# Up-projections of a two-layer encoder on one Trainium2 core: the product of the activation moved to VectorE, weight sums and sums of squares made by adding transfers

## The chip, the cores and the metric

The kernel runs on one core of a Trainium2 chip. The metric is the device time of one execution in microseconds, as a median of several runs. The engines are TensorE (PE in the rows, its weight loads PEld), VectorE (DVE), ScalarE (ACT), GpSimd (POOL) and SyncE (SP), which issues transfers. They run side by side, each in the order of its own queue.

## The reference

The input is `x`, 1024 frames of 1024 channels in float32. Two layers run over it; each adds a mixer and then a gated feed-forward network to the residual stream. The feed-forward network is what the change touches:

```python
def conv_ffn(h, w_up, conv_w, conv_b, w_down):       # h: 1024 x 1024, w_up: 1024 x 5632
    u = h @ w_up
    up = jnp.pad(u, ((0, 0), (CONV_WIDTH - 1, 0), (0, 0)))
    conv = conv_b
    for j in range(CONV_WIDTH):                       # width 3, causal, per channel
        conv = conv + conv_w[j] * up[:, j:j + s]
    a, g = jnp.split(conv, 2, axis=-1)                # 2816 channels each
    return (jax.nn.silu(a) * g) @ w_down
```

`h` is the residual stream after an RMS norm with a gain per channel. The mixer of layer 0 is stick-breaking attention beside a pooling mixer, that of layer 1 gated linear attention.

## The kernel before

Everything lies channels on partitions: a tile of `x` is 128 channels by 1024 frames, and there are 8 of them. Matmuls work on pairs of float32r tiles: a float32 value is cut into a high part (ScalarE, a cast) and a remainder (VectorE, a subtraction), and a product takes three matmuls, high x high, high x low, low x high. Such a cut is called a split.

*The feed-forward loop.* The 5632 up-projected channels are 22 pairs of tiles, one of `a` and one of `g`. The first two pairs are plain projections. From the third on a pair is computed in `class Pair` by a scheme of seven half-size products instead of eight: the weights of the pair and the input are 2 x 2 blocks, and the products P1 to P7 use blocks and sums of blocks. Each product is 12 matmuls of 128x512, 84 for a pair. On the weight side four sums of 128x512 are formed per pair (lines 856, 857, 860 and 861, in `sum12` and `sum34`): `s12[:, T0]`, the two halves of `raw_g` added; `s12[:, T1]`; `s34[:, T0]`; and `s34[:, T1]`, where `T0` and `T1` are the two 512-column halves. They are split into `s12h`, `s12l`, `s34h`, `s34l`; `a22` is the split of one half of `raw_g`, and `whi`, `wlo` that of `wraw` (lines 843, 844). On the input side four sums per channel block are formed once per layer by `rsums` (lines 905 to 908) and split by `rblock`.

The products accumulate in four PSUM banks, named `lin`, `z`, `t` and `d`. ScalarE copies intermediate results out (lines 926, 933, 941), VectorE adds them to others (lines 937, 942, 948, 952) and scales the outputs `u` by the norm's factor (line 911). P3 goes on accumulating in the bank that line 942 has read, so P3 waits for line 942; P7 goes on in the bank that the copy of line 933 has read. Then come the convolution (line 956 on ScalarE, 957 and 959 on VectorE), the SiLU on ScalarE (line 1076), the product with the gate on GpSimd (line 1077) and a store of the result to DRAM. Three tiles `c` serve the two convolutions of a pair in turn. The loads, sums and splits for a pair are made ahead, in the iterations before it (`load_a`, `sum12`, `sum34`, called after the products of the pair).

*The entry.* The last two blocks of the mixer's output projection are added to the residual tiles by `add_tiles` (line 819) in the order `ORDER`, two tiles ahead; for each finished tile `NormBlocks.add` stores it, makes two split blocks (`blk`, lines 289 and 290), squares it (line 309, `ndg` or `nsq` in the rows) and adds the square to `nacc` on VectorE (line 310). The first up-projection of the layer (`first_tile`) runs two tiles behind, between the `add_tiles`. At the end PE sums the squares over channels (`stats`, line 261), ScalarE and VectorE make the factor, VectorE spreads it on a diagonal (line 268), and after the plain projection of tile 1 PE spreads it over the partitions (`spread`, line 275). The outputs of the first projections can only be scaled after that (line 1008).

*The order.* PE runs in the order in which the program names its instructions. All other engines and SP's queue are put in order by a planner, which works through the program's dependences with assumed costs; on the chip that order is fixed. A buffer with several turns is handed on when its last reader is done. The tiles in `xpool` have 11 places: the 8 residual tiles, the sums of squares, temporaries.

Of the kernel before, what the change touches and what calls it, by code (L numbers as in the profile page):

```python
# [56 lines left out]
def trunk_kernel(  # L57
# [220 lines left out]
    class NormBlocks(Norm):  # L278
# [14 lines left out]
        def add(self, m, x):  # L293
            xs[m] = dram.tile([P, T], F32, tag=f"xs{self.layer}_{m}", name="xs")
            nc.sync.dma_start(xs[m], x)
            g = pcol(self.col + m)
            if m < KT // 2:
                self.b11.append(self.block(x[:, 0:512], g))
                self.b12.append(self.block(x[:, 512:T], g))
            else:  # L300
                self.b21.append(self.block(x[:, 0:512], g))
                self.b22.append(self.block(x[:, 512:T], g))
            self.n += 1
            if self.n == 1:
                self.acc = self.acc_tile()
                S.activation(self.acc, x, AF.Square)
            else:
                sq = self.sq_tile()
                S.activation(sq, x, AF.Square)
                V.tensor_tensor(self.acc, self.acc, sq, op=ALU.add)  # L310
            if m < KT // 2:
                S.activation(x, x, AF.Copy, scale=g)
# [514 lines left out]
    def ffn(layer, nm, after, ow, mixt, onward=None):  # L827
# [23 lines left out]
        def load_a(i):  # L851
            raws[i], *A[i] = raw_a(i)
            nc.sync.dma_start(raw_g, wup[layer, FT + i])

        def sum12(i):
            V.tensor_tensor(s12[:, T0], raw_g[:, T0], raw_g[:, T1], op=ALU.add)
            V.tensor_tensor(s12[:, T1], s12[:, T0], raws[i][:, T0], op=ALU.subtract)

        def sum34(i):
            V.tensor_tensor(s34[:, T0], raws[i][:, T0], raw_g[:, T0], op=ALU.subtract)  # L860
            V.tensor_tensor(s34[:, T1], raws[i][:, T1], s12[:, T1], op=ALU.subtract)
# [26 lines left out]

        rhs = {n: [None] * 4 for n in ("T1", "T2", "T3", "T4")}
# [12 lines left out]
        def rsums(k):  # L902

            lo_, hi_, g = x[k], x[k + 4], pcol(nm.col + k + 4)
            V.tensor_tensor(lo_[:, T0], lo_[:, T1], lo_[:, T0], op=ALU.subtract)
            V.scalar_tensor_tensor(lo_[:, T1], hi_[:, T1], g, lo_[:, T1], op0=ALU.mult, op1=ALU.subtract)
            V.scalar_tensor_tensor(hi_[:, T1], hi_[:, T1], g, lo_[:, T0], op0=ALU.mult, op1=ALU.subtract)
            V.scalar_tensor_tensor(hi_[:, T0], hi_[:, T0], g, hi_[:, T1], op0=ALU.mult, op1=ALU.subtract)
# [53 lines left out]

        first = []
# [16 lines left out]
        def plain(i, tags):  # L980
            w, ps = raw_a(i)[1:], [bank(t) for t in tags]
            for n in range(KT):
                plain_tile(w, ps, n)
            return ps

        otags = itertools.cycle("td")
        add_tiles(ow, mixt, otags, ORDER[:2])
        for n, m in enumerate(ORDER):
            if n >= 2:
                add_tiles(ow, mixt, otags, [m])  # L990
            nm.add(m, x[m])
            if n >= 2:
                first_tile(n - 2)
# [4 lines left out]
        first_tile(KT - 2)  # L998
        first_tile(KT - 1)
        nm.stats("t")  # L1000
        ps = plain(1, "td")
        nm.spread(iter("dt"))
# [12 lines left out]
        load_a(2)  # L1015
        split_a22()
        sum12(2)
        sum34(2)
# [16 lines left out]
        for i in range(FT):  # L1035
# [8 lines left out]
            else:  # L1044
                p = Pair(i)
                ua, ug = p.ua, p.ug
                if not nx:
                    first_down()
                p.P1()
                p.P5()  # L1050
                p.P6()
                if nx:
                    split_s12()
# [4 lines left out]
                p.P7()  # L1058
                scaled(ug[:, T1], T1)
# [3 lines left out]
                if nx:  # L1063
                    split_a22()
                scaled(ug[:, T0], T0)
                p.P3()
                if nx:
                    split_s34()
                scaled(ua[:, T1], T1)
            if 0 < i < FT - 2:  # L1070
                load_a(i + 2)
                sum12(i + 2)
                sum34(i + 2)
# [3 lines left out]
            G.tensor_tensor(ca, ca, cg, op=ALU.mult)  # L1077
# [393 lines left out]
```

## Time and profile before

| | |
|---|---|
| median of three runs | 2269.87 us (2266.28 to 2270.54) |
| the profiled execution's own time | 2268.67 us |
| its span, first to last instruction | 2267.0 us |
| PE busy | 2210.9 us (98%) |
| DVE busy | 1644.5 us (73%) |
| ACT busy | 1009.3 us (45%) |
| POOL busy | 305.1 us (13%) |
| mean granted TensorE clock | 0.995 |

The profile is of one execution. Times in its rows count from the start of the span. A busy PE is not PE at its peak, since matmuls overlap; how fast it goes is read from the starts of its instructions. Idle time of an engine that nobody waits for costs nothing. The feed-forward loop of layer 0 lies at about 485 to 894 us, that of layer 1 at 1614 to 2024.

### The profile page before, as it was taken

How to read it: one execution, taken by the hardware profiler on the slowest of the kernel's cores; microseconds unless marked ns; L12 is line 12 of the kernel's file. 1: busy time of each engine (PE TensorE's matmuls, PEld its weight loads, DVE VectorE, ACT ScalarE, POOL GpSimd, SP SyncE). 2: the span in 40 equal slices, each digit the busy share in tenths (PEclk: the TensorE clock that was granted, in tenths of full speed). 3: DMA queues.
4: the chain of work that ended last, by engine and by line, in shares of the span. 5: the costliest groups of instructions: out<-in, count | busy, mean ns of one | idle time of the engine just before them, and what ended most of it. 6: DMA issues, size and time to landing. Idle time of an engine off the chain costs nothing.

```text
span 2267.0 us, 27398 instructions
## 1 busy us (share of the span) xinstructions
PE 2210.9 (98%) x10648; PEld 1822.6 (80%) x10648; DVE 1644.5 (73%) x2244; ACT 1009.3 (45%) x1533; POOL 305.1 (13%) x191
## 2 busy tenths in 40 slices
PE   8999989999999999999999999999999999999999
PEld 7889868777888887888887788787778888878887
DVE  5687688799999998554546555548899999985543
ACT  6666666454444444221256253536544444442210
POOL 2230110001111112321000000000011111133210
PEclk9999999999999999999999999999999999999999
DMA  4132341222222226421101011102222222264312
GB/s 144 58 103 77 110 137 53 107 78 75 84 84 84 84 84 221 151 96 53 30 21 45 29 47 38 47 29 103 75 83 78 81 84 84 84 224 138 102 47 75
DMA packets 56898, 194.26 MB, mean 86 GB/s; under 512 B 6832, under 2 KB 7472, under 8 KB 56768
## 3 DMA queue, kind: packets, MB, share of 16 engines
q1 hardware_dynamic: 56768, 192.51, 26.3%
q8 instruction: 84, 1.38, 0.3%
q14 instruction: 46, 0.38, 0.1%
HBM read 149.49 MB, written 42.99 MB: 85 GB/s over the span
## 4 chain that ended last, share of the span: by engine, by line
PE 83%; DVE 6%; ACT 4%; issue 4%; DMA 2%; POOL 1%; SPq 0%; DVEq 0%; ACTq 0%; POOLq 0%
PE lin L885 13%; PE z L885 9%; PE lin L137 5%; PE lin L139 5%; PE lin L141 5%; PE t L885 4%; PE d L885 4%; PE z L137 3%; PE z L139 3%; PE z L141 3%; PE t L137 3%; PE t L139 3%; PE t L141 3%; PE d L137 2%; PE d L139 2%
## 5 line engine op out<-in xcount | busy, mean ns | idle before, releaser
L123 ACT CAST whi<-wraw 128x1024 fp32r<-128x1024 f32 (+3 forms) x106 | 105.4, 996 | 355.2 <-PE d L139 222.2
L1077 POOL TENSOR_TENSOR c<-c 128x1024 f32<-128x1024 f32 x44 | 109.5, 2490 | 900.5 <-ACT c L1076 884.5
L911 DVE TENSOR_TENSOR u<-u,rstd_bc 128x512 f32<-128x512 f32 x160 | 159.8, 1000 | 2.6
L124 DVE TENSOR_TENSOR wlo<-wraw,whi 128x1024 fp32r<-128x1024 f32 (+2 forms) x92 | 130.5, 1418 | 38.8 <-ACT whi L123 38.2
L956 ACT ACTIVATE c<-u,prm 128x1024 f32<-128x1024 f32 x88 | 109.6, 1245 | 76.5 <-DVE u L911 75.0
L1106 POOL TENSOR_TENSOR act<-a,act 128x1024 fp32r<-128x1024 f32 x40 | 107.1, 2685 | 218.3 <-ACT act L1105 214.2
L137 PE MATMUL lin<-h_hi,whi 128*128 128x512 f32 x304 | 119.9, 433 | 6.3 <-ACT whi L123 6.1
L819 DVE TENSOR_TENSOR x<-x,t 128x512 f32<-128x512 f32 x105 | 71.9, 685 | 64.6 <-PE t L141 64.3
L959 DVE SCALAR_TENSOR_TENSOR c<-u,prm,c 128x1022 f32<-128x1022 f32 x88 | 118.3, 1344 | 0.1
L675 DVE TENSOR_TENSOR_SCAN pt<-pt,z 128x128 f32<-128x128 f32 (+3 forms) x96 | 93.1, 970 | 33.7 <-ACT z L668 32.6
L957 DVE SCALAR_TENSOR_TENSOR c<-u,prm,c 128x1023 f32<-128x1023 f32 x88 | 112.5, 1279 | 6.5 <-ACT c L956 6.4
L885 PE MATMUL d<-T,a 128*128 128x512 f32 x480 | 115.3, 389 | 0.0
L819 DVE TENSOR_TENSOR x<-x,d 128x512 f32<-128x512 f32 x105 | 71.9, 684 | 56.6 <-PE d L141 56.6
L139 PE MATMUL lin<-h_lo,whi 128*128 128x512 f32 x304 | 109.7, 399 | 1.8 <-DVE h_lo L247 1.8
L141 PE MATMUL lin<-h_hi,wlo 128*128 128x512 f32 x304 | 109.6, 399 | 0.0
L885 PE MATMUL z<-blk,s34h 128*128 128x512 f32 x320 | 100.7, 396 | 5.7 <-DVE u L942 5.7
L885 PEld LDWEIGHTS d<-T,a 128*128 128x128 f32 x480 | 90.1, 188 | 18.7
L864 ACT CAST s12h<-s 128x1024 fp32r<-128x1024 f32 x42 | 44.2, 1052 | 135.2 <-PE lin L885 120.3
L885 PE MATMUL lin<-T,s34h 128*128 128x512 f32 x320 | 98.9, 390 | 2.2 <-ACT tm L933 2.2
L885 PE MATMUL z<-blk,s12h 128*128 128x512 f32 x320 | 100.7, 396 | 0.0
L885 PE MATMUL lin<-blk,whi 128*128 128x512 f32 x320 | 99.8, 393 | 0.0
L885 PE MATMUL lin<-T,s12h 128*128 128x512 f32 x320 | 99.5, 392 | 0.0
(429 smaller groups left out, 6334.4 us busy)
## 6 DMA issues: line engine op xcount, KB each, us to landing
wraw<-in_wup SPq DMA_DIRECT2D x44, 512.0 KB, 3.6
act<-c SPq DMA_DIRECT2D x44, 512.0 KB, 2.6
wraw<-in_wdn SPq DMA_DIRECT2D x44, 512.0 KB, 3.9
raw_g<-in_wup SPq DMA_DIRECT2D x40, 512.0 KB, 3.6
a<-act SPq DMA_DIRECT2D x40, 512.0 KB, 4.5
xs<-x SPq DMA_DIRECT2D x16, 512.0 KB, 2.6
x<-xs SPq DMA_DIRECT2D x16, 512.0 KB, 5.0
x<-in_xT SPq DMA_DIRECT2D x8, 512.0 KB, 5.0
```

The costliest lines, as they stand in the source:

```text
L124: (eng or V).tensor_tensor(lo[:, cs], raw[:, cs], hi[:, cs].bitcast(F32), op=ALU.subtract)
L137: PE.matmul(out[i], wh, ah[i], start=first, stop=False)
L139: PE.matmul(out[i], wh, al[i], start=False, stop=False)
L141: PE.matmul(out[i], wl, ah[i], start=False, stop=last)
L819: V.tensor_tensor(x[m][:, cs], x[m][:, cs], pss[m][i], op=ALU.add)
L885: PE.matmul(ps, w, m, start=first and k == 0 and n == 0, stop=k == 3 and n == 2, skip_group_check=True)
L911: V.tensor_tensor(dst, dst, rstd_bc[:, cs], op=ALU.mult)
L956: S.activation(c, u, AF.Identity, scale=pcol(b + 2), bias=pcol(b + 3))
L957: V.scalar_tensor_tensor(c[:, 1:], u[:, :T - 1], pcol(b + 1), c[:, 1:], op0=ALU.mult, op1=ALU.add)
L959: V.scalar_tensor_tensor(c[:, 2:], u[:, :T - 2], pcol(b), c[:, 2:], op0=ALU.mult, op1=ALU.add)
L1077: G.tensor_tensor(ca, ca, cg, op=ALU.mult)
L1106: G.tensor_tensor(t[1], a32, t[0].bitcast(F32), op=ALU.subtract)
```

## The change

Five things change. (1) The product of the activation (line 1077) goes from GpSimd to VectorE. (2) Two of the four weight sums per pair are made by transfers that add to their target, issued from GpSimd's queue: `s12[:, T0]` is loaded with one half of the weights and the other half is added from DRAM; `s34[:, T1]` is loaded with a half and `s12[:, T1]` is added from on-chip memory. (3) To let these be plain additions, the sign of `s12[:, T1]` is turned round, and on the input side the signs in `rsums` with it, with a small tile `ngain` of negated gains. (4) The loads, sums and splits for coming pairs are placed anew, spread over the products of a pair. (5) In the entry, five of the sums of squares are made by adding transfers into one tile, which joins the accumulator at the end; three tiles instead of two are computed ahead; and the spread of the norm's factor goes into the middle of the plain projection.

```diff
@@ NormBlocks.add
+            sq = self.acc_tile() if self.n == 1 else self.sq_tile()
+            S.activation(sq, x, AF.Square)
             if self.n == 1:
-                self.acc = self.acc_tile()
-                S.activation(self.acc, x, AF.Square)
+                self.part = sq
+            elif self.n < KT - 1:
+                G.dma_start(self.part, sq, accum_op=ALU.add)
+            elif self.n == KT - 1:
+                self.acc = sq
             else:
-                sq = self.sq_tile()
-                S.activation(sq, x, AF.Square)
                 V.tensor_tensor(self.acc, self.acc, sq, op=ALU.add)
+                V.tensor_tensor(self.acc, self.acc, self.part, op=ALU.add)
@@ ffn
+        def load_s1(i):
+            nc.sync.dma_start(s12[:, T0], wup[layer, FT + i][:, T0])
+            G.dma_start(s12[:, T0], wup[layer, FT + i][:, T1], accum_op=ALU.add)
+
+        def load_g(i):
+            nc.sync.dma_start(raw_g, wup[layer, FT + i])
+
         def load_a(i):
-            raws[i], *A[i] = raw_a(i)
-            nc.sync.dma_start(raw_g, wup[layer, FT + i])
-
-        def sum12(i):
-            V.tensor_tensor(s12[:, T0], raw_g[:, T0], raw_g[:, T1], op=ALU.add)
-            V.tensor_tensor(s12[:, T1], s12[:, T0], raws[i][:, T0], op=ALU.subtract)
-
-        def sum34(i):
+            raws[i] = wpool.tile([P, T], F32, tag="wraw", name="wraw", bufs=1)
+            nc.sync.dma_start(raws[i], wup[layer, i])
+
+        def load_s4(i):
+            nc.sync.dma_start(s34[:, T1], wup[layer, i][:, T1])
+
+        loads = (load_s1, load_g, load_a, load_s4)
+
+        def sums(i):
+            V.tensor_tensor(s12[:, T1], raws[i][:, T0], s12[:, T0], op=ALU.subtract)
+            G.dma_start(s34[:, T1], s12[:, T1], accum_op=ALU.add)
             V.tensor_tensor(s34[:, T0], raws[i][:, T0], raw_g[:, T0], op=ALU.subtract)
-            V.tensor_tensor(s34[:, T1], raws[i][:, T1], s12[:, T1], op=ALU.subtract)
+
+        def split_a11(i):
+            A[i] = [wpool.tile([P, T], R32, tag=n, name=n) for n in ("whi", "wlo")]
+            split(*A[i], raws[i])
...
+        ngain = small.tile([P, 4], F32, tag="ngain", name="ngain", bufs=1)
+        S.activation(ngain, prm[:, nm.col + 4:nm.col + 8], AF.Copy, scale=-1.0)
@@ rsums
-            V.scalar_tensor_tensor(hi_[:, T1], hi_[:, T1], g, lo_[:, T0], op0=ALU.mult, op1=ALU.subtract)
-            V.scalar_tensor_tensor(hi_[:, T0], hi_[:, T0], g, hi_[:, T1], op0=ALU.mult, op1=ALU.subtract)
+            V.scalar_tensor_tensor(hi_[:, T1], hi_[:, T1], ng, lo_[:, T0], op0=ALU.mult, op1=ALU.add)
+            V.scalar_tensor_tensor(hi_[:, T0], hi_[:, T0], g, hi_[:, T1], op0=ALU.mult, op1=ALU.add)
@@ entry of ffn
+        AHEAD = 3
-        def plain(i, tags):
+        def plain(i, tags, amid=None):
             w, ps = raw_a(i)[1:], [bank(t) for t in tags]
             for n in range(KT):
                 plain_tile(w, ps, n)
+                if n == 4 and amid is not None:
+                    amid()
             return ps
...
-        add_tiles(ow, mixt, otags, ORDER[:2])
+        add_tiles(ow, mixt, otags, ORDER[:AHEAD])
         for n, m in enumerate(ORDER):
-            if n >= 2:
+            if n >= AHEAD:
                 add_tiles(ow, mixt, otags, [m])
             nm.add(m, x[m])
-            if n >= 2:
-                first_tile(n - 2)
+            if n >= AHEAD:
+                first_tile(n - AHEAD)
...
-        first_tile(KT - 2)
-        first_tile(KT - 1)
+        for n in range(KT - AHEAD, KT):
+            first_tile(n)
         nm.stats("t")
-        ps = plain(1, "td")
-        nm.spread(iter("dt"))
+        ps = plain(1, "td", lambda: nm.spread(iter("dt")))
...
-        load_a(2)
+        for ld in loads:
+            ld(2)
         split_a22()
-        sum12(2)
-        sum34(2)
+        sums(2)
+        split_a11(2)
         split_s12()
         split_s34()
@@ the loop over pairs
+                further = i + 2 < FT
                 p.P1()
+                if nx:
+                    sums(i + 1)
                 p.P5()
                 p.P6()
-                if nx:
-                    split_s12()
                 p.P2()
                 scaled(ua[:, T0], T0)
                 if not nx:
                     p.P4()
                 p.P7()
+                if nx:
+                    split_s12()
+                if further:
+                    load_s1(i + 2)
                 scaled(ug[:, T1], T1)
                 if nx:
                     p.P4()
                 p.D21()
                 if nx:
                     split_a22()
+                if further:
+                    load_g(i + 2)
                 scaled(ug[:, T0], T0)
+                if nx:
+                    split_a11(i + 1)
+                if further:
+                    load_a(i + 2)
                 p.P3()
                 if nx:
                     split_s34()
+                if further:
+                    load_s4(i + 2)
                 scaled(ua[:, T1], T1)
-            if 0 < i < FT - 2:
-                load_a(i + 2)
-                sum12(i + 2)
-                sum34(i + 2)
+            if i == 1:
+                for ld in loads:
+                    ld(i + 2)
             conv(FT + i, ug, cg)
             conv(i, ua, ca)
             S.activation(ca, ca, AF.Silu)
-            G.tensor_tensor(ca, ca, cg, op=ALU.mult)
+            V.tensor_tensor(ca, ca, cg, op=ALU.mult)
```

## Rows read from the trace of the kernel before

**Rows 1.** The page, busy time of the engines: microseconds, share of the span, instructions.

```profile
PE 2210.9 (98%) x10648; PEld 1822.6 (80%) x10648; DVE 1644.5 (73%) x2244; ACT 1009.3 (45%) x1533; POOL 305.1 (13%) x191
```

**Rows 2.** Busy time by stage: the stretch, its length, then for PE, PEld, DVE, ACT and POOL the busy microseconds and the number of instructions, then the granted TensorE clock, the busy share of the transfer engines and their GB/s. The first is the entry of layer 0, the second the middle of its loop, the third the end of layer 1's entry.

```profile
424.00:485.00 61.00, 58.45 (x257) 46.51 (x255) 59.23 (x83) 39.67 (x52) 0.00 (x0) 1.00 0.26 95
540.00:870.00 330.00, 330.00 (x1439) 269.95 (x1438) 304.93 (x343) 150.83 (x174) 40.86 (x17) 1.00 0.26 85
...
1591.00:1600.00 9.00, 7.14 (x25) 5.38 (x24) 9.00 (x13) 7.15 (x11) 0.00 (x0) 0.81 0.35 117
```

**Rows 3.** Waits of PE from 424 to 900 us (entry and loop of layer 0): who waited for whom, microseconds in total, times, longest.

```profile
PE z L885 <- DVE u L942: 2.9, 3, 1.4
PE lin L139 <- DVE blk L290: 2.0, 2, 1.2
PE lin L885 <- ACT tm L933: 1.1, 1, 1.1
PE lin L137 <- DVE u L1008: 0.8, 1, 0.8
```

**Rows 4.** Waits of PE from 1557 to 2030 us (entry and loop of layer 1), the same columns. The two lines left out are, word for word, the last two of rows 3.

```profile
PE lin L139 <- DVE blk L290: 3.4, 2, 1.9
PE z L885 <- DVE u L942: 2.7, 2, 1.4
...
```

**Rows 5.** Waits of the weight loads (PEld) from 424 to 900 us, the same columns.

```profile
PEld z L885 <- DVE u L942: 4.2, 3, 1.8
PEld lin L139 <- DVE blk L290: 2.9, 2, 1.7
PEld lin L137 <- DVE u L1008: 1.6, 1, 1.6
PEld lin L885 <- ACT tm L933: 1.5, 1, 1.5
```

**Rows 6.** The timeline of a steady pair of layer 0: start, duration, engine, line, operation, output and inputs, count. The two weight-load rows are the first of P3 in this pair and in the next.

```profile
607.57 2.40 POOL L1077 TENSOR_TENSOR c<-c 128x1024 f32<-128x1024 f32 x1 [17.03 <-ACT c L1076]
...
608.36 2.16 DVE L911 TENSOR_TENSOR u<-u,rstd_bc 128x512 f32<-128x512 f32 x1
...
610.44 1.21 DVE L844 TENSOR_TENSOR wlo<-wraw,whi 128x1024 fp32r<-128x1024 f32 x1
611.57 0.68 DVE L942 TENSOR_TENSOR u<-tm,z 128x512 f32<-128x512 f32 x1
...
612.66 0.41 PEld L885 LDWEIGHTS z<-blk,s34h 128*128 128x128 f32 x2
...
618.27 0.68 DVE L856 TENSOR_TENSOR s<-raw_g 128x512 f32<-128x512 f32 x1
618.88 1.22 DVE L865 TENSOR_TENSOR s34l<-s,s34h 128x1024 fp32r<-128x1024 f32 x1
...
631.95 0.41 PEld L885 LDWEIGHTS z<-blk,s34h 128*128 128x128 f32 x2
```

**Rows 7.** The timeline of POOL, DVE and ACT around the first pair of seven products in layer 0, the same columns; in brackets how long the engine stood before it and for whom.

```profile
499.89 3.29 POOL L1077 TENSOR_TENSOR c<-c 128x1024 f32<-128x1024 f32 x1 [157.96 <-ACT c L1076]
...
500.84 3.43 DVE L959 SCALAR_TENSOR_TENSOR c<-u,prm,c 128x1022 f32<-128x1022 f32 x1
...
504.36 1.06 ACT L1076 ACTIVATE c<-c 128x1024 f32<-128x1024 f32 x1 [4.07 <-DVE c L959]
...
511.20 2.40 POOL L1077 TENSOR_TENSOR c<-c 128x1024 f32<-128x1024 f32 x1 [8.02 <-DVE c L959]
...
511.57 3.11 DVE L844 TENSOR_TENSOR wlo<-wraw,whi 128x1024 fp32r<-128x1024 f32 x1
```

**Rows 8.** Groups of instructions by line: line, engine, operation, output and inputs, count, then busy microseconds, mean nanoseconds of one, and idle time before them.

```profile
L911 DVE TENSOR_TENSOR u<-u,rstd_bc 128x512 f32<-128x512 f32 x160 | 159.8, 1000 | 2.6
...
L310 DVE TENSOR_TENSOR nacc<-nacc,ndg 128x1024 f32<-128x1024 f32 x7 | 8.6, 1226 | 0.0
...
L864 ACT CAST s12h<-s 128x1024 fp32r<-128x1024 f32 x42 | 44.2, 1052 | 135.2 <-PE lin L885 120.3
```

**Rows 9.** Transfers by line: tile and source, queue, count, size of one, median microseconds from issue to landing.

```profile
wraw<-in_wup SPq DMA_DIRECT2D x44, 512.0 KB, 3.6
...
x<-xs SPq DMA_DIRECT2D x16, 512.0 KB, 5.0
...
out_yT<-x SPq DMA_DIRECT2D x16, 256.0 KB, 2.0
```

**Rows 10.** The timeline of the entry of layer 0, columns as in rows 6: the squares of the second and the sixth tile (ACT), the last addition of squares (DVE), the first matmul of the plain projection, the diagonal of the norm's factor (DVE).

```profile
431.87 1.04 ACT L309 ACTIVATE ndg<-x 128x1024 f32<-128x1024 f32 x1
...
452.47 1.05 ACT L309 ACTIVATE ndg<-x 128x1024 f32<-128x1024 f32 x1
...
466.69 1.22 DVE L310 TENSOR_TENSOR nacc<-nacc,ndg 128x1024 f32<-128x1024 f32 x1
...
471.53 0.48 PE L137 MATMUL t<-blk,whi 128*128 128x512 f32 x1
...
475.23 1.22 DVE L268 TENSOR_TENSOR ndg<-ident,rstd_tok 128x1024 f32<-128x1024 f32 x1
```

More of the change, by code (lines that the diff above doesn't have):

```diff
@@ L902, in rsums @@
         def rsums(k):
-            lo_, hi_, g = x[k], x[k + 4], pcol(nm.col + k + 4)
+            lo_, hi_, g, ng = x[k], x[k + 4], pcol(nm.col + k + 4), ngain[:, k:k + 1]
             V.tensor_tensor(lo_[:, T0], lo_[:, T1], lo_[:, T0], op=ALU.subtract)
             V.scalar_tensor_tensor(lo_[:, T1], hi_[:, T1], g, lo_[:, T1], op0=ALU.mult, op1=ALU.subtract)
-            V.scalar_tensor_tensor(hi_[:, T1], hi_[:, T1], g, lo_[:, T0], op0=ALU.mult, op1=ALU.subtract)
-            V.scalar_tensor_tensor(hi_[:, T0], hi_[:, T0], g, hi_[:, T1], op0=ALU.mult, op1=ALU.subtract)
+            V.scalar_tensor_tensor(hi_[:, T1], hi_[:, T1], ng, lo_[:, T0], op0=ALU.mult, op1=ALU.add)
+            V.scalar_tensor_tensor(hi_[:, T0], hi_[:, T0], g, hi_[:, T1], op0=ALU.mult, op1=ALU.add)
         def scaled(dst, cs):
```

## The prediction, made before the change was run

> **What bounds the kernel now.** The engine line of the page comes first: TensorE (PE) is busy 2210.9 us of a span of 2267.0 us [rows 1], so all other engines together can give back at most 56 us, and only where PE stands. The stage table says where that is: in the long middle of each feed-forward loop PE is busy 330.0 us of 330.0, while the entry of layer 0 has 58.45 of 61.00 and layer 1's entry has a stretch of 9 us with 7.14 us busy at a granted clock of 0.81 [rows 2]. So the steady loop has nothing to give as long as its pace stays, and it can only lose; the entries and the ends of the loops can give. PE's waits name what stands there: in layer 0 a block (`blk`, line 290), the first scaled outputs (line 1008), the copy of `u2` (line 933) and the sum of line 942 [rows 3]; layer 1 repeats the same four with nearly the same numbers [rows 4]. These are small: 6.8 and 8.0 us. The weight-load row sees the same waits somewhat longer, because a weight load normally runs ahead of its matmul [rows 5].
>
> The steady pair shows why VectorE (DVE) matters. The pair's P3 product starts at 612.66 and the next one's at 631.95, a period of 19.29 us [rows 6]. In it DVE is busy 304.93/330 x 19.29 = 17.8 us [rows 2, 6], so it has 1.5 us to spare. And one instruction of it is not its own time: POOL's product runs from 607.57 for 2.40 us, and DVE's scaling that starts at 608.36 takes 2.16 us, until POOL is done, where a sum of the same size takes 0.68 (618.27) [rows 6]. All 160 scalings average 1000 ns [rows 8]. In the steady loop this is absorbed: line 942 runs at 611.57, P3 starts at 612.66 and PE does not wait. In the first pair it is not. There POOL's products at 499.89 and 511.20 fall on DVE instructions that take 3.43 and 3.11 us; behind the first ScalarE stands 4.07 us, and behind the second comes line 942 [rows 7]. Those are the waits on lines 933 and 942 of [rows 3].
>
> **The change, part by part.**
>
> *The product on DVE.* POOL loses 2.40 us a pair, DVE gains one 128x1024 instruction: 1.13 us from start to start, as from 610.44 to 611.57 [rows 6]. DVE loses the stretched scaling, 2.16 - 0.68 = 1.48 us.
>
> *Two of four sums as adding transfers.* DVE loses two 128x512 instructions at 0.61 us from start to start (618.27 to 618.88) [rows 6], 1.2 us. Together DVE falls to 17.8 + 1.1 - 1.5 - 1.2 = 16.2 us a pair; its spare time grows from 1.5 to 3.1 us. In the steady loop that buys nothing, since PE does not wait there.
>
> *The price of an adding transfer.* No row shows one. Plain 256 KB takes 2.0 us to land, 512 KB takes 3.6 to 5.0 [rows 9]. An adding one must read its target as well; I bound it by the plain 256 KB row below, 2.0, and twice the 5.0 of 512 KB above, 10.0. I take 4.0 for 256 KB (twice the 2.0 of its own size) and 5.0 to 7.2 for 512 KB (the slower row, or twice the faster one).
>
> *Where it can hurt in the loop.* The adding load of `s12` follows the split of `s12`, which now comes after P7. If it begins at about 611.0, shortly before line 942, it is through by 613.2 (1.05 us for the cast [rows 8], 1.13 us for the remainder); 2.0 us for the plain half gives 615.2; 4.0 us for the adding half gives 619.2. `sums` stands after P1 of the next pair; seven products take 19.29 us, 2.76 each, and P3 begins at 612.66 [rows 6], so P1 behind it ends near 618.2. So DVE waits about 1.0 us there if the planner puts `sums` as early as the program does. Behind it on DVE are the convolution of the pair before, the sums of product outputs and line 942, for which P3 waits. 1.0 us is inside the spare 3.1, so I cost it at nothing; the cover is gone when the adding half takes over 6.1 us. The data itself is not late at either bound: at 5.0 + 10.0 it lands by 628.2, and the split that needs it runs near 630. POOL's queue has only adding transfers in the loop, so nothing else stands behind their waits. SP's queue gets two more loads a pair, and the store of the activation stands behind them; the next pair's first convolution instruction on ScalarE reuses that tile.
>
> *Transfers.* A pair moves 1.5 MB now (two loads and a store of 512 KB) and about 2.5 MB after, adding included. The queues' share, 0.26 in the steady loop [rows 2], becomes about 0.26 x 2.5 / 1.5 = 0.43, or 0.5 if the adding bytes count twice: still room.
>
> *The entries.* Five of seven additions of squares (1226 ns each [rows 8]) leave DVE; it gets one more at the end: with the two that stay that is 7 down to 2, 6.1 us less in a stretch where DVE is busy 59.23 of 61.00 [rows 2]. One more tile is also computed ahead, so each block has one tile of projection, 12 matmuls or 2.8 us (84 matmuls take 19.29 us, 0.23 each), more before PE reads it. The two block waits of each layer are 0.8 to 1.9 us each [rows 3, 4]: both are covered. The squares are added one after the other into one tile: the second square is there at 432.9, the sixth at 453.5 [rows 10]. With t per transfer the chain ends at the later of 432.9 + 5t and 453.5 + t, and the sum is wanted at 466.7 [rows 10]. At 5.0 it ends at 458.5, at 7.0 about in time, at 10.0 at 482.9, 16 us late.
>
> *The spread of the norm* moves into the middle of the plain projection, after 30 of its 48 matmuls: 471.5 + 30 x 0.23 = 478.4. Its input is there at 475.23 + 1.22 = 476.5 [rows 10], so PE does not wait for it, and the waits on line 1008 go (0.8 us by matmul, 1.6 us by weight load [rows 3, 5]).
>
> *The rest* (one tiny ScalarE instruction for the negated gains, signs turned round in `rsums`, splits and loads in another order) has the same instructions; ScalarE is busy 39.67 of 61.00 us in the entry [rows 2], which covers the one that is new.
>
> **The sum.** Waits that go, by matmul: layer 0, 2.0 + 0.8 + 1.1 + 1.5 = 5.4 us, the 1.5 being line 942 without its longest wait of 1.4, which lies in the last pair, where the order of products leaves nothing between P7 and P3, and which stays [rows 3]. Layer 1: 3.4 + 0.8 + 1.1 + 1.3 = 6.6 us [rows 3, 4]. The clock: after the 1.9 us wait in layer 1's entry the 9 us stretch was granted 0.81 [rows 2]; 0.19 x 9 = 1.7 us come back if PE does not stand there. Lower sum 13.7 us. By weight loads layer 0 has 2.9 + 1.6 + 1.5 + (4.2 - 1.8) = 8.4 us [rows 5], 1.56 times as much; the same factor makes 18.7 us of both layers, with the clock 20.4. Between them lie 17 us. I take off 1.13 us a layer for the product, which now stands in the same crowded first pair of [rows 7]: 14.7 us. The profiled execution took 2268.67 us (span 2267.0 and 1.7 outside it), 1.2 us under the median of 2269.87, so I carry the difference over: 2269.9 - 14.7 = **2255 us**, with a range of its own of 2250 to 2262.
>
> **A rule against it.** In the steady loop POOL's instruction and DVE's exclude each other for 1.5 us [rows 6]; whether POOL's writing of transfer descriptors is held up by DVE no row shows, since the transfers are issued by SP [rows 9]. The Trainium skill, page "SBUF — State Buffer", section "SBUF: two separate sides", speaks against issuing from GpSimd beside a busy VectorE: descriptors wait while VectorE runs a two-port mode, and one transfer measured there went from about 620 ns to about 3100 ns. The same page, section "Who interferes with whom", says that `tensor_tensor` has no such mode, and most of this loop's VectorE instructions are of that kind or its scalar form. If the rule held all the same, its 2.5 us on top of my 4.0 would make an adding load of 6.5 us, 0.4 us over the cover, and an estimate of 2255 + 40 x 0.4 = 2271 us.
>
> **The rivals.**
>
> *Slower: DVE stands at `sums` in every pair.* From 6.1 us per adding half load on, the rest goes to P3 in each of 40 pairs: 40 us for each us. At 7.0 it is 36 us, 2291 us; at 6.6, 2275. For it: 7.0 lies between the bounds, DVE runs in order, and the planner has no row to go by. Against it: 4.0 is nearer to the rows of that size, and the planner may put `sums` later, where the data allow some 11 us more. This is the mechanism that the rule above would work by. Chance 0.20.
>
> *No change: the chain of squares is late.* Above t = 7 each us makes the chain 5 us later in each entry, and PE stands at the norm's statistics, since it issues in order. At t = 8.2 that is 6 us twice, and of 14.7 some 3 are left: 2267 us. For it: twice the slower 512 KB row is 10.0. Against it: source and target are both on chip here. It includes that the waits just move elsewhere in the entry. Chance 0.18.
>
> *More: every wait of the changed parts goes as the weight loads show it,* 20.4 us, and some pace with it: below 2250 us. Chance 0.10.
>
> *The forecast* has 0.52.
>
> **The numbers.** A difference under 0.2% (4.5 us) is about what a measurement of this kernel cannot tell from none. Faster: 0.52 + 0.10 = 0.62; same 0.18; slower 0.20. The range from 2246 to 2284 leaves out the faster half of the third rival's cases at most and somewhat over half of the slower ones.
>
> **What would show it.** Right: no POOL instruction in the loop; DVE near 277 us of a steady 330; scalings all near 0.68; the waits on lines 290, 933 and 1008 of before gone, line 942's left in the last pair alone; no stretch of low clock in layer 1's entry; the steady period still 19.29. The slower rival would show as DVE waiting for the transfer into `s` in every pair, with P3 behind it; the second as the statistics waiting for `nacc`. The prediction is wrong as well if PE's pace in the steady pair moves: 1% of it is 0.19 x 40 = 8 us.

## The result: slower, 2277.8 us

The changed kernel takes 2277.82 us (median of 7), the kernel before 2268.82 beside it: a ratio of 1.0044, interval 1.0035 to 1.0054. Its profiled execution took 2276.27 us, span 2274.6. First the page's engine line and four lines of its list of transfers (tile and source, queue, count, size, median microseconds to landing):

```profile
PE 2221.6 (98%) x10648; PEld 1813.1 (80%) x10648; DVE 1584.1 (70%) x2198; ACT 1006.6 (44%) x1535; POOL 271.9 (12%) x237
...
s<-in_wup SPq DMA_DIRECT2D x80, 256.0 KB, 2.7
...
s<-in_wup POOLq DMA_DIRECT2D x40, 256.0 KB, 4.0
s<-s POOLq DMA_DIRECT2D x40, 256.0 KB, 3.9
...
nacc<-ndg POOLq DMA_DIRECT2D x5, 512.0 KB, 4.6
nacc<-nsq POOLq DMA_DIRECT2D x5, 512.0 KB, 5.6
```

VectorE has 60 us less to do than in [rows 1], PE 11 us more. The same stretches as in [rows 2]:

```profile
424.00:485.00 61.00, 60.17 (x266) 48.21 (x265) 54.51 (x79) 40.94 (x55) 7.05 (x8) 1.00 0.63 168
540.00:870.00 330.00, 328.48 (x1402) 260.74 (x1402) 272.11 (x318) 145.94 (x168) 28.58 (x33) 1.00 0.51 135
1591.00:1600.00 9.00, 7.53 (x31) 5.47 (x30) 5.28 (x9) 6.75 (x9) 0.86 (x1) 1.00 0.71 180
```

In the entry of layer 0 PE is busy longer. The stretch that had a granted clock of 0.81 has 1.00; but so it has in a second trace of the kernel before (before_again, below), so this cannot be put down to the change:

```profile
1591.00:1600.00 9.00, 7.12 (x31) 5.51 (x30) 9.00 (x13) 7.89 (x11) 0.00 (x0) 1.00 0.48 176
```

In the 330 us of the steady loop, though, PE begins 1402 matmuls where it began 1439: most of the loss is in the loop. Waits from 424 to 900 us, of VectorE first, then of the weight loads, to set beside [rows 5]:

```profile
DVE s L875 <- DMA s<-in_wup: 46.0, 18, 3.5
...
PEld z L905 <- DVE u L964: 7.7, 16, 1.8
PEld lin L905 <- ACT tm L948: 6.5, 14, 1.0
```

VectorE stands 18 times, 2.6 us each, at the difference of `sums` (line 875) for the adding load, and two waits of PE come with it. Line 964 is line 942 of before, line 948 is 933, line 933 is the scaling of line 911. One such pair in the timeline (start, duration, engine, line; in brackets the idle time before it and for whom):

```profile
687.49 0.69 DVE L933 TENSOR_TENSOR u<-u,rstd_bc 128x512 f32<-128x512 f32 x1
687.51 0.30 PEld L905 LDWEIGHTS z<-blk,s34h 128*128 128x128 f32 x2 [0.43 <-DVE u L964]
690.64 0.69 DVE L875 TENSOR_TENSOR s<-wraw,s 128x512 f32<-128x512 f32 x1 [2.45 <-DMA s<-in_wup]
...
692.45 0.68 DVE L933 TENSOR_TENSOR u<-u,rstd_bc 128x512 f32<-128x512 f32 x1
...
693.16 1.24 ACT L978 ACTIVATE c<-u,prm 128x1024 f32<-128x1024 f32 x1 [5.24 <-DVE u L933]
...
695.26 0.57 ACT L948 COPY tm<-lin 128x512 f32<-128x512 f32 x1
695.88 0.30 PEld L905 LDWEIGHTS lin<-T,s12h 128*128 128x128 f32 x2 [0.19 <-ACT tm L948]
...
701.69 1.22 DVE L885 TENSOR_TENSOR s12l<-s,s12h 128x1024 fp32r<-128x1024 f32 x1
702.93 0.33 SPq L859 DMA_DIRECT2D s<-in_wup  x1
706.35 0.87 POOL L860 DMA_DIRECT2D s<-in_wup  x1 [4.73 <-DVE wlo L885]
...
710.55 0.69 DVE L875 TENSOR_TENSOR s<-wraw,s 128x512 f32<-128x512 f32 x1 [2.70 <-DMA s<-in_wup]
```

Line 875 comes directly behind the pair's second scaling (687.49), as the planner put it; the data are there 3.1 us after P3 has begun (687.51). The third scaling (692.45), behind it, is late, so ScalarE's convolution (line 978) stands 5.24 us, the copy of line 948 comes behind that, and PE waits for the copy. The load that feeds line 875 is issued by SP at 702.93, its adding half by POOL at 706.35, and VectorE goes on at 710.55: 7.6 us. POOL's bracket names VectorE, but in 37 of the 40 loads of this run POOL issues 0.55 to 0.58 us after the plain half has landed, so that is what it waits for.

The span by stretches, each from weight load to weight load (attention ends where `add_tiles` begins; an entry ends with the first of the seven products, a loop with the last):

| us | attention | entry 0 | loop 0 | down 0 | mixer 1 | entry 1 | loop 1 | rest |
|---|---|---|---|---|---|---|---|---|
| before | 422.81 | 73.61 | 390.55 | 233.98 | 428.91 | 77.60 | 390.19 | 249.35 |
| before, second trace | 422.94 | 73.64 | 390.94 | 233.94 | 431.76 | 75.98 | 390.18 | 249.32 |
| after | 421.38 | 70.96 | 396.54 | 234.83 | 429.71 | 74.82 | 395.95 | 250.42 |

Of the 7.6 us between the spans the loops are +11.7, the entries -5.4, the down stages (the last column is that of layer 1 with the end) +1.9, attention and mixer 1 together -0.6. The first pair of seven products fell from 22.17 to 19.53 us in layer 0 and from 22.23 to 20.58 in layer 1; the rest of the loops costs 8.6 and 7.4 us more. So the parts that were to give did give 9.7 us (5.4 in the entries, 4.3 in the first pairs), and the other pairs took 16.0. Pairs without a stall take 19.38 where [rows 6] have 19.29, the others up to 20.6. So there are two losses: the stalls, and a pace that is 0.5% slower where nothing waits.

### The profile page after: what moved, and what is told of

It reads as the page before. It is cut to its first block, busy times and chain, and to the rows that moved or that the text cites. A ratio compares the mean times of both kernels' runs of the same rounds, so it can differ in the third digit from the quotient of the medians.

```text
span 2274.6 us, 27814 instructions
## 1 busy us (share of the span) xinstructions
PE 2221.6 (98%) x10648; PEld 1813.1 (80%) x10648; DVE 1584.1 (70%) x2198; ACT 1006.6 (44%) x1535; POOL 271.9 (12%) x237
## 5 line engine op out<-in xcount | busy, mean ns | idle before, releaser
L933 DVE TENSOR_TENSOR u<-u,rstd_bc 128x512 f32<-128x512 f32 x160 | 109.5, 686 | 1.3
L905 PE MATMUL t<-blk,whi 128*128 128x512 f32 x320 | 99.6, 392 | 0.0
L876 POOL DMA_DIRECT2D s<-s x40 | 34.5, 862 | 522.7 <-DVE c L979 410.6
```

Of the source, the lines that this page charges most:

```text
L905: PE.matmul(ps, w, m, start=first and k == 0 and n == 0, stop=k == 3 and n == 2, skip_group_check=True)
L933: V.tensor_tensor(dst, dst, rstd_bc[:, cs], op=ALU.mult)
```

## The experiments

All times are medians of 4 to 11 executions beside the kernel before on the same chip (2267.6 to 2269.6 us). Loops and pairs are read from one trace of each run, layer 0 first; a steady pair is the mean of the second to the eighteenth of a loop, or the one value that nearly all of them have.

| run | us | ratio to before | interval | loops | steady pair |
|---|---|---|---|---|---|
| after | 2277.82 | 1.0044 | 1.0035 to 1.0054 | 396.5, 396.0 | 19.8, 19.7 |
| sums_behind | 2269.52 | 1.0002 | 0.9994 to 1.0011 | 390.8, 389.7 | 19.38 |
| s12_dve | 2267.62 | 0.9999 | 0.9991 to 1.0008 | 390.1, 392.2 | 19.45, 19.57 |
| p_dve | 2275.00 | 1.0030 | 1.0017 to 1.0042 | 394.4, 396.7 | 19.67, 19.75 |
| entry | 2272.62 | 1.0021 | 1.0011 to 1.0031 | 394.5, 395.9 | 19.70, 19.65 |
| p_dve_pin | 2260.39 | 0.9963 | 0.9950 to 0.9975 | 387.9, 387.6 | 19.29 |
| both_pin | 2256.39 | 0.9944 | 0.9930 to 0.9958 | 387.6, 387.8 | 19.29 |
| ngain | 2273.79 | 1.0026 | 1.0016 to 1.0036 | 392.5, 391.8 | 19.38 |
| ngain_64b | 2256.80 | 0.9957 | 0.9941 to 0.9974 | 388.3, 388.3 | 19.19 |
| ngain_96b | 2271.50 | 1.0021 | 1.0011 to 1.0030 | 391.3, 391.0 | 19.33 |
| ngain_256b | 2268.94 | 1.0002 | 0.9992 to 1.0012 | 390.3, 390.4 | 19.29 |
| after_256b | 2278.31 | 1.0043 | 1.0031 to 1.0056 | 395.4, 393.6 | 19.76, 19.61 |
| sums_behind_256b | 2263.11 | 0.9975 | 0.9966 to 0.9984 | 388.7, 388.2 | 19.29 |
| sums_behind_64b | 2251.98 | 0.9930 | 0.9916 to 0.9943 | 386.9, 387.1 | 19.19 |
| both_pin_64b | 2246.64 | 0.9901 | 0.9888 to 0.9915 | 385.7, 385.6 | 19.19 |

**Line 875 held back (sums_behind).** Theory: its place in VectorE's order. Rival: the transfers' traffic.

```diff
                 if nx:
-                    sums(i + 1)
+                    with tc.issue_after(done.ins):   # done: last VectorE step of conv(FT + i)
+                        sums(i + 1)
```

> The changed kernel with one difference: the two VectorE instructions of `sums` are issued behind the convolution of the pair before, some 8 us later in VectorE's order; no transfer and no instruction is taken away. Theory A (order): in the changed kernel VectorE stands 89.8 us at `sums` for the adding load, ScalarE's convolution and copy queue up behind it, and P6 and P3 wait; the steady pair went from 19.29 to about 19.8 us, 0.4 of it by these waits, 0.1 by a slower pace. Then VectorE's wait for the transfer goes to near 0, the steady pair to about 19.4, and the time to 2278 - 38 x 0.4 = about 2263 us. Theory B (traffic): the pair is slower because the transfer engines are twice as busy (share 0.26 to 0.51) and PE's reads suffer; then the pair stays at 19.7 to 19.8 and the time at 2275 to 2280 us.

The loops lose 12.0 us with every transfer still there. The middle of the loop:

```profile
540.00:870.00 330.00, 330.00 (x1432) 268.51 (x1432) 282.08 (x325) 148.34 (x171) 28.51 (x33) 1.00 0.51 138
```

PE never waits, at the same transfer share of 0.51. The stalls were the order: the pair is that of theory A, not that of B. The time is not: 2269.5 and not 2263, since the loops gave 12.0 us and not 15, and in this trace the entries (+1.5 and +1.8) and the mixer of layer 1 (+4.2) are longer than in after. The pair stays at 19.38, so the pace was something else.

**The adding load undone (s12_dve):** VectorE makes `s12[:, T0]` from `raw_g`, as before; the second adding transfer stays.

> The changed kernel with the sum of the two halves of `raw_g` back on VectorE: the plain load and the adding load of `s12` are gone (0.5 MB a pair less), one 128x512 instruction more on VectorE; the adding transfer into `s34` stays. Theory A: VectorE no longer waits for an adding load, the steady pair comes to about 19.4, the time to about 2263 us. Theory B: a third to a half of the added traffic goes, the share falls to about 0.4, the pair to about 19.6, the time to about 2270 us.

Without that transfer there is nothing to stand for, and the loops return nearly (392.2 in layer 1, where P3 still waits 9 times for line 964). The time, 2267.6, and the pairs lie between the two theories, and traffic fell with the transfer, so this run alone does not part them; sums_behind does, and it says that in the loop the transfer hurt only through the place at which VectorE asked for it.

**The product alone (p_dve)** and **the entries alone (entry)**, each on the kernel before.

> The kernel before with the product on VectorE alone. Theory A (the first pair's waits come from GpSimd's product standing in VectorE's way): the waits on the copy and the sum in the first pair go, 2 to 3 us a layer, the steady pair stays 19.29: about 2264 us. Rival: the first pair is late for another reason and the product's 1.13 us come on top in VectorE's order: 2268 to 2272 us.

> The kernel before with the changes of the entry alone (squares by adding transfers, three tiles ahead, the spread in the middle of the plain projection). In the changed kernel the first pair begins 4.1 us earlier in layer 0. Theory A: the entry is all gain: 4 us in layer 0 and 3 to 4 us in layer 1, about 2261 us. Rival: the chain of adding transfers (4.6 to 5.6 us each) takes part of it back in layer 1: 2264 to 2268 us.

Both are misses. The wished-for gains are there (first pairs of 19.57 in p_dve, entries of 70.8 and 73.3 in entry), and both lose more in the loop. 1.7 us of p_dve's loop 0 is a stretch at a lower granted clock (0.66 from 555 to 560 us); beside it one wait has grown in both, which 424 to 900 us of the kernel before show 3 times [rows 5]; first p_dve, then entry, whose line 946 is line 942:

```profile
PEld z L885 <- DVE u L942: 11.0, 20, 2.5
```

```profile
PEld z L889 <- DVE u L946: 11.8, 20, 1.9
```

The run entry changes no line of the loop. What moved is the planner's order: before, the last weight sum (line 861) stands between the two steps of the second convolution (lines 957 and 959):

```profile
602.51 1.28 DVE L957 SCALAR_TENSOR_TENSOR c<-u,prm,c 128x1023 f32<-128x1023 f32 x1
...
604.31 0.69 DVE L861 TENSOR_TENSOR s<-wraw,s 128x512 f32<-128x512 f32 x1
604.91 1.28 DVE L959 SCALAR_TENSOR_TENSOR c<-u,prm,c 128x1022 f32<-128x1022 f32 x1
```

In both of these it stands behind both steps. In entry (line 963 is line 959, 865 is 861):

```profile
605.79 1.28 DVE L963 SCALAR_TENSOR_TENSOR c<-u,prm,c 128x1022 f32<-128x1022 f32 x1
606.99 0.69 DVE L865 TENSOR_TENSOR s<-wraw,s 128x512 f32<-128x512 f32 x1
```

p_dve's timeline, one pair:

```profile
624.78 1.28 DVE L959 SCALAR_TENSOR_TENSOR c<-u,prm,c 128x1022 f32<-128x1022 f32 x1
625.97 0.69 DVE L861 TENSOR_TENSOR s<-wraw,s 128x512 f32<-128x512 f32 x1
...
626.69 0.33 SPq L840 DMA_DIRECT2D wraw<-in_wup  x1
...
630.40 1.05 ACT L843 CAST whi<-wraw 128x1024 fp32r<-128x1024 f32 x1 [2.84 <-DMA wraw<-in_wup]
...
631.49 1.23 DVE L844 TENSOR_TENSOR wlo<-wraw,whi 128x1024 fp32r<-128x1024 f32 x1 [1.23 <-ACT whi L843]
632.63 0.68 DVE L942 TENSOR_TENSOR u<-tm,z 128x512 f32<-128x512 f32 x1
...
633.36 0.30 PEld L885 LDWEIGHTS z<-blk,s34h 128*128 128x128 f32 x2 [0.40 <-DVE u L942]
```

The weight tile has one buffer; line 861 is its last reader, and 0.03 us after its end SP loads the next. From there the chain runs without a gap through load, cast and split to line 942, for which P3 waits (633.36): 6.7 us from the start of line 861 to that of line 942, where the kernel before has 7.3 (604.31 and 611.57 in [rows 6]) and PE does not wait. The chain is a ring that closes in each pair. That the order costs the time is shown by holding it:

**The order pinned (p_dve_pin, both_pin).** The sums are put ahead of the second convolution.

```diff
-                sum34(i + 2)
+                last = sum34(i + 2)          # returns its last VectorE step, line 861
             conv(FT + i, ug, cg)
-            conv(i, ua, ca)
+            with tc.issue_after(last.ins):
+                conv(i, ua, ca)
```

> The kernel before with the product on VectorE, and VectorE's queue pinned: in each pair the last weight sum of the next pair (line 861) is issued ahead of the second convolution (line 957), two places earlier than in the run p_dve. Theory 'the order': in p_dve the sum of line 861 ended 1 to 2 us later in the pair than before, so the load of the weight tile (line 840), its rounding (line 843) and its split (line 844) came late, the output sum behind the split (line 942) too, and P3 waited. Pinned, line 861 ends where it did before: pairs of 19.29, first pairs 19.6, loops of about 388 us (394.4 and 396.7 in p_dve, 390.6 and 390.2 before), in all 2263 (2261 to 2266). Rival 'the product's 1.2 us on VectorE': the pairs stay at 19.5 to 19.7 and the time at 2273 to 2276.

> The same pinned kernel with the changed entries too (squares by adding transfers, three output tiles ahead, the spread in the midst of a product); all loads and sums of the loop stay as before. Theory 'the order': the entries give 2.7 us each as in every run with that code (73.6 to 70.9 and 77.7 to about 74), the loops 2.5 us each through their first pair: 2257.5 (2255 to 2262). Rival 'the planner undoes it elsewhere' (the run entry gained 2.8 and 4.3 us in the entries and lost 3.9 and 5.7 in loops whose code was untouched): 2266 to 2273, with P3 waiting for line 946.

Both came as the order theory says, p_dve_pin even lower. Lines 861 and 942 of it now lie 7.9 us apart, 1.2 more than the ring needs, and PE does not wait:

```profile
617.86 0.69 DVE L861 TENSOR_TENSOR s<-wraw,s 128x512 f32<-128x512 f32 x1
...
625.74 0.69 DVE L942 TENSOR_TENSOR u<-tm,z 128x512 f32<-128x512 f32 x1
```

So the product on VectorE is worth 2.6 us a layer if the order is held. The entry of layer 0 gives 2.9 (70.76 for 73.65 in p_dve_pin), that of layer 1 nothing here (74.85 for 74.88; more on it below). Of both_pin's 13 us, 4 lie in the attention (418.92), which nothing changed.

**The pace (ngain and its widths).** All kernels with the small tile of negated gains had pairs of 19.38. Here it alone is added, unread, to the kernel before.

```diff
+        ngain = small.tile([P, 4], F32, tag="ngain", name="ngain", bufs=1)   # 16, 32, 64 wide below
+        S.activation(ngain, prm[:, nm.col + 4:nm.col + 8], AF.Copy, scale=-1.0)
```

> The kernel before with only the small tile of negated gains and its one ScalarE instruction for each layer, which nothing reads. Theory 'addresses': the slower pace of the products P2 and P7 (2.77 us where before has 2.73), of the pair (19.38 for 19.29) and of the down stage (234.8 for 234.0) comes with where the tiles lie, which this tile shifts: pairs of 19.38, down stage 234.8, in all 2271 to 2273. Rival 'transfers or the new instructions': nothing moves, pairs of 19.29 and 2268 within 1.

> The run ngain with the unread tile of 16 bytes a partition (which takes 32) widened to 256 bytes, so that everything behind it lies a multiple of 256 bytes from its place in the kernel before. The order of every engine is the same. Theory 'addresses': pairs back at 19.29 (19.38 in ngain), P2 and P7 at 2.73 (2.77), the down stage of layer 0 at 234.0 (234.8), loops 390.5, in all 2268 to 2270 (2273.8 in ngain). Rival 'the extra instruction or the order it leaves': 19.38, 234.8 and 2273 stay.

> The run ngain with the unread tile widened to 64 bytes a partition, so that everything behind it lies 64 bytes further than in the kernel before (32 in ngain, 256 in ngain_256b). Same order on every engine. If a multiple of 64 bytes is what the slow products want: pairs of 19.29, P2 and P7 at 2.73, down stage of layer 0 at 234.0, and 2268 to 2270. If it must be 128 or 256: pairs of 19.38, 2.77, 234.8 and 2272 to 2274.

> The same with 96 bytes a partition. If a multiple of 64 bytes is wanted: pairs of 19.38, P2 and P7 at 2.77, down stage 234.8, 2272 to 2274, as in ngain with 32. If it was only the place of ngain itself that was bad: 19.29 and 2268 to 2270.

The orders of VectorE, ScalarE (but for the new instruction), GpSimd and SyncE are those of the kernel before in all four. The steady loop of ngain, then of ngain_64b:

```profile
540.00:870.00 330.00, 330.00 (x1432) 268.55 (x1431) 302.44 (x341) 150.18 (x172) 40.99 (x17) 1.00 0.26 85
```

```profile
540.00:870.00 330.00, 330.00 (x1446) 271.15 (x1445) 307.49 (x344) 151.56 (x173) 40.77 (x17) 1.00 0.27 87
```

PE never waits, at clock 1.00, and begins 1432 matmuls or 1446, where [rows 2] have 1439; only the place of the tiles differs:

| shift of the tiles behind, bytes a partition (by the widths; no address was read) | 0 | 32 | 64 | 96 | 256 |
|---|---|---|---|---|---|
| pair | 19.29 | 19.38 | 19.19 | 19.33 | 19.29 |
| down stage of layer 0 | 233.98 | 234.82 | 230.75 | 234.80 | 233.94 |

The address theory is right in its main point: 256 gives back what 32 took. The rule that I tried, multiples of 64, fails: 64 is not as good as 0 but better. The times miss a little (ngain 2273.8 for 2271 to 2273) or, for 64 bytes, by 11 us. I had not expected that any place beats that of the kernel before.

**Do the two add up?** (after_256b, sums_behind_256b, sums_behind_64b, both_pin_64b)

> The run sums_behind (the changed kernel with VectorE's difference of line 875 held behind the first convolution) with the tile of negated gains widened in the same way. Theory 'order and addresses are the whole loss': pairs of 19.29 in place of 19.38, so 1.7 us off each loop, 0.9 off the down stage of layer 0 and 1.1 off the stage at the end: about 5.3 off 2269.5, so 2264 (2262 to 2267), faster than the kernel before. Rival 'the adding transfers cost pace': pairs of 19.38 and 2268 to 2271.

> The changed kernel, its order untouched, with the tile of negated gains widened to 256 bytes: the missing corner of four (VectorE's order as planned or held back; 32 or 256 bytes of shift). If order and addresses add up: 2277.8 - 6.4 = 2271.4 (2270 to 2273), unstalled pairs of 19.29, the waits for the transfer into s (line 875) as before in about 17 of 19 pairs. If the stalls hide the faster pace, or the pace hides the stalls: 2275 to 2278.

> The run sums_behind with the tile of negated gains at 64 bytes. By the run ngain_64b (11.0 us under the kernel before, against ngain_256b at +0.5): 2263.1 - 11.5 = 2251.6 (2249 to 2255), pairs of 19.19, down stage of layer 0 at 230.8. If the place that is good for the kernel before is not good for the changed one: 2262 to 2270.

> The run both_pin (the kernel before with the product on VectorE, the changed entries and VectorE's order pinned, no adding transfer in the loop) with an unread tile of 64 bytes. If the two causes add up: 2256.4 - 11 = 2245 (2242 to 2249), pairs of 19.19. If the adding transfers of the loop cost nothing by themselves, sums_behind_64b lies above it only by its first pairs (about 1 us each) and by layer 1's entry (1.7 us); if they cost pace, its pairs are longer than 19.19.

Three came as expected in time and pairs, after_256b 7 us too high. In the loops the four corners do add up: both loops together take 792.5 us (after), 789.1 (after_256b), 780.5 (sums_behind), 776.9 (sums_behind_256b), so the order is worth 12.0 or 12.2 and the place 3.4 or 3.6; the down stages of after_256b also give 1.8 us. Those of sums_behind_256b give only 0.9: layer 1's keeps the slower pace (its last stretch takes 250.36 us, 250.40 in sums_behind), though the tile is as wide as in after_256b (249.45). So the width alone does not set the pace there; why is open. What is missing in after_256b lies in its attention, 427.34 us against 421.38, with the same instructions in the same order. Three stretches of it, after first:

```profile
84.00:100.00 16.00, 15.87 (x99) 13.77 (x98) 11.35 (x22) 11.02 (x23) 1.32 (x1) 1.00 0.01 3
240.00:253.00 13.00, 12.22 (x67) 10.26 (x66) 9.79 (x20) 9.18 (x21) 2.40 (x1) 1.00 0.48 162
253.00:290.00 37.00, 35.95 (x209) 30.75 (x209) 25.07 (x51) 24.13 (x51) 2.92 (x2) 0.95 0.29 82
```

```profile
84.00:100.00 16.00, 15.89 (x86) 13.40 (x85) 11.17 (x22) 9.55 (x20) 0.00 (x0) 0.89 0.03 12
240.00:253.00 13.00, 11.41 (x54) 9.11 (x53) 8.88 (x17) 9.01 (x20) 3.95 (x2) 0.87 0.33 101
253.00:290.00 37.00, 35.98 (x197) 30.68 (x196) 23.18 (x47) 21.37 (x44) 2.67 (x2) 0.91 0.32 96
```

Its granted clock is lower in all three, part of each stretch at 1.2 instead of 2.4 GHz, and it begins 13, 13 and 12 matmuls fewer. Over the whole attention 20.5 us are at 1.2 GHz and 10.2 in after; half of the difference, 5.1 us, is most of the 6.0. The mean clock of the timed executions agrees: 0.995 in the median for after_256b, 0.997 for after; 0.002 of 2275 us is 4.6 us. Whether that comes with the shift or by chance stays open. For chance speaks that the two other runs at 256 bytes have 421.56 (ngain_256b) and 421.22 (sums_behind_256b), and that the second trace of the kernel before also has 0.89 where its first had 1.00 (84 to 100 us), and 1.00 where the first had 0.91 (253 to 290).

sums_behind_64b and both_pin_64b both have steady pairs of 19.19, with and without adding transfers in the loop: these cost no pace.

```profile
540.00:870.00 330.00, 330.00 (x1446) 271.11 (x1446) 285.13 (x326) 150.52 (x174) 28.50 (x33) 1.00 0.52 140
```

```profile
540.00:870.00 330.00, 330.00 (x1446) 271.15 (x1445) 301.55 (x357) 151.63 (x172) 0.00 (x0) 1.00 0.27 89
```

The loops differ only by the first pair (20.83 and 21.02 against 19.50 and 19.49). Layer 1's entry is not 1.7 us longer in sums_behind_64b, as expected, but 1.4 shorter (72.93 and 74.28; the trace of both_pin_64b has a stretch of low clock there). both_pin_64b is 0.99 of the kernel before.

**The second trace of before (before_again).**

> The kernel before once more, for a second trace of it: how far do the stretches whose code no change touches (attention up to the first entry, 422.8; the mixing layer of layer 1, 428.8) differ between two executions of one kernel? If by under 0.5 us, the 421.4 to 426.0 and 427.3 to 433.8 of the other kernels are differences of order; if by several us, they say nothing.

Attention agrees to 0.13 us, but the mixer of layer 1 differs by 2.9 and the entry behind it by 1.6 (table above). So these two can be read to about 3 us, the loops and down stages of one kernel to under 0.5. The attention, the same code everywhere, spreads more between kernels: 418.6 to 427.3 us, and 6.0 between after and after_256b, whose order is the same.

Layer 1's entry differs by a stretch at 1.2 GHz, which comes and goes. With the old code of the entry four traces of eight have it (77.56 to 77.60 us) and four do not (74.88 to 76.03); with the new code four of nine have it (74.28 to 76.60) and five do not (72.93 to 74.82). Like with like, the new entry of layer 1 is 2.0 us shorter in the mean, and the stretch costs 1.8 to 1.9. The entry of layer 0 takes 73.6 in the mean with the old code and 71.2 with the new.

## Why the prediction was wrong

It said 2255 us, the median is 2277.8, inside the range of 2246 to 2284 but on the other side of no change. By its own steps:

*Right: what the product does to VectorE.* All scalings take 679 to 695 ns, where [rows 8] have a mean of 1000, and VectorE's busy time came to 16.6 us a pair (282.08 of 330 in sums_behind, at 19.38) for 16.2 forecast. The first pair lost its stall (2.6 and 1.7 us; p_dve 2.6 in both layers). The Trainium skill, page "SBUF — State Buffer", section "Who interferes with whom", says that a VectorE instruction with two on-chip inputs contends with a GpSimd instruction that reads on-chip memory. The trace agrees: 2.16 us for the scaling that begins beside GpSimd's product [rows 6], 0.68 in the timeline above.

*Right: the adding transfer's price.* 4.0 and 3.9 us for 256 KB against 4.0 taken, 4.6 and 5.6 for 512 KB against 5.0 to 7.2. The plain half was taken too low: 2.7, not 2.0, and the 0.6 us from its landing to the issue of the adding half were not in the sum. The Trainium skill, page "SBUF — State Buffer", section "SBUF: two separate sides", says that descriptors written by GpSimd wait while VectorE is in a two-port mode. The 2.5 us that the prediction worked out from it do not show: 4.0 us, with VectorE busy 272 of 330 us; that tests the rule for this loop's instructions alone. The chain of squares was in time: its last adding transfer is issued at 457.74, the last sum (line 314) begins at 464.0.

*Failed: "1.0 us is inside the spare 3.1, so I cost it at nothing".* Two things were wrong. The place: I took `sums` where the program has it, behind P1, 5.5 us after P3's start; the planner put it behind the second scaling, some 0.7 us after P3's start, so the wait was 2.6 us and not 1.0. (The data came earlier than I had them, 3.1 us after P3's start and not 6.5, since the load began earlier; VectorE asked earlier still.) And the cover: spare time is a sum over the whole pair, but a wait hits the instruction that is next in the queue. Behind line 875 stood a scaling, behind that in ScalarE's queue a convolution and a copy that PE needs, with under 2.6 us to give. So a wait inside the spare 3.1 still cost 0.3 to 0.4 us in a mean pair, 12.0 us in both loops (after against sums_behind). My rival "DVE stands at `sums` in every pair" named the place and the chain, but tied it to a price over 6.1 us; it came at 4.0.

*Failed: "the steady period still 19.29".* I named a moved pace as something that would make the prediction wrong, 8 us for 1%, but gave it no term in the sum and no cause. It was 0.5%, and cost 0.09 us a pair and 0.9 to 1.1 in each down stage, 5.5 us in all (3.6 by the loops of the two runs with the order held), through 32 bytes of a tile that I had filed under "the rest".

*Half right: the entries.* The waits on line 1008 went, those on line 290 fell to 0.3 us (weight loads) in layer 0 and 0.9 (matmuls) in layer 1, and the trace has no low clock in layer 1's entry. That last is luck: the stretch comes and goes with the old code and with the new, so the term of 1.7 us for the clock was not the change's to give. The entries gave 2.7 and 2.8 us, near the matmuls' count in layer 0 (2.8), but not the 5.9 of layer 1; like with like it is 2.0 there. The step from the lower sum of 13.7 us to the middle at 17, by the longer waits of the weight loads, is not borne out: entries and first pairs together gave 9.7. One new wait stands in each (0.8 and 1.6 us, `add_tiles`, with the third tile ahead).

*Not foreseen at all:* that an edit in one place re-orders VectorE's queue in another. The run entry shows it bare. And the rest of the 14.7 us: with the order held and 256 bytes the changed kernel takes 2263.1, and the forecast's sign is right; 5.3 us beside the kernel before. In its trace the entries give 3.7 (layer 1's has the stretch of low clock: 76.57, where sums_behind_64b has 72.93 without it) and the first pairs 3.4, the last stretch takes back 1.0, and attention and mixer 1 together 1.5. Why its first pairs (20.79 and 20.19) are over 19.5 is open.

## What to carry to other kernels

Spare time of an in-order engine is no cover for a wait: look at the instruction behind the wait, and at who needs it, in the planned order and not in the program's. Where a planner sets the order, compare the order of the hot loop before and after any edit, also one elsewhere, and pin the one or two places on which a ring of buffers hangs. Before a pace is ascribed to new work, try the old work at shifted addresses: here an unread tile moved the whole kernel from +0.26% to -0.43%.

## What the hardware showed that I had not expected

Matmuls of the same shape and order go at a pace that depends on where their tiles lie: 19.19 to 19.38 us for 84 of them, 230.75 to 234.82 us in the down stage, for shifts of 0 to 256 bytes. Neither the tile nor the mechanism was found, and one down stage kept the slower pace at a width at which it is fast elsewhere. An adding transfer of 256 KB costs 4.0 us from issue to landing against 2.7 for a plain one, the same from DRAM and from on-chip memory, and GpSimd is busy 0.87 us issuing it.
